# Hybrid decoder layer on one core: both halves of four convolution tiles on one weight, the triangular inverse over fewer elements, compressed probabilities two heads at a time, the second norm's sums taken from PSUM

## The chip, the cores and the metric

The kernel runs on one core of a Trainium2 chip. The metric is the device time of one execution in microseconds (us). The engines are named as the profile names them: PE is TensorE's matmul queue and PEld its weight loads, DVE is VectorE, ACT is ScalarE, POOL is GpSimd, SP is SyncE, whose queue (SPq) issues nearly all DMA transfers. Each engine runs its instructions in order.

## The reference, cut to what matters

One layer over 1024 tokens of width 1024, in float32:

```python
h = rmsnorm(x, norm_mix)
q, kv, gate, qkv_gdn, z, b, a = split(h @ w_in)
o_nsa = rmsnorm(nsa_mixer(q, kv, gate, ...), nsa_norm)   # 8 heads, 2 key/value heads, width 64
o_gdn = gdn_mixer(qkv_gdn, z, b, a, ...)                 # 4 heads, width 128, chunks of 64
x = x + concat([o_nsa, o_gdn]) @ w_out
u = causal_dwconv(rmsnorm(x, norm_ffn) @ ffn_up, ffn_conv)     # width 2 x 2816
x = x + (silu(u_gate) * u_up) @ ffn_down
return rmsnorm(x, norm_final)

# in nsa_mixer, for each query and head: compressed, selected and window attention
o = gate_c * (p_cmp @ vc) + gate_s * (p_sel @ v_sel) + gate_w * (p_win @ v_win)
# in gdn_mixer: q, k, v = split(silu(causal_dwconv(qkv, conv_w))); for each chunk of 64 tokens
a_mat = tril(kb @ k.T * decay, -1)
sol = triangular_solve(a_mat + eye, [vb, kb * exp(g)])   # then a recurrence from chunk to chunk
```

`vc` and the compressed keys have 63 rows (blocks of 32 tokens at a stride of 16), so a compressed probability row has 64 columns here.

## The kernel before, in words

Matrix products keep float32 accuracy by splitting each operand into a high part (ScalarE, a cast) and a low part (the rest, GpSimd or VectorE), and by three products high x high, high x low, low x high (`mm3`, L126 to L128; `mm_more`, L1116). `split_weight` loads 128 x 1024 weights as w_raw and makes w_h on ScalarE (L116) and w_l on GpSimd (L118).

The order on each engine is that of the program text, except that blocks of the program marked with a high priority are moved ahead by the scheduler. The stages, in us of the profiled span:

- to 110: first norm, values and gates, first convolution blocks.
- 110 to 440: `conv_block` (one for each of 12 tiles of 128 channels and each half of 512 tokens, L463 to L469: matmuls into proj_ps, ScalarE copies, three taps and a gate on VectorE) beside gated DeltaNet. DeltaNet goes by pairs of token tiles (4 pairs): `gdn_blocks` (L339 to L355) inverts the 32 x 32 triangular blocks of a pair (2 tiles, 4 blocks, 4 heads) on VectorE. It loads the blocks as bb through DRAM (d_blk), starts from zinit and does 31 passes, each a multiplication into ztmp (L348) and an addition into zb (L350). The 128 partitions are 32 blocks times 4, and each holds 8 of the 32 rows of its inverse; `na` of them take part in pass j. zb goes to DRAM (d_z) and from there to Zx (`gdn_solve`), with which TensorE goes on to the recurrence (L408 to L419).
- 440 to 775: attention in 16 units (8 token tiles, 2 key/value heads). Scores (s_ps, L809, L811), softmax, transposes of the probabilities (pt, L877), copies of these (pT, L880, L882), and products with the values into one tile po of PSUM (L890), which has one buffer and is copied to oT by ScalarE (L893). A unit's compressed probabilities pc are the first of its jobs.
- 775 to 800: output projection and residual (`phase_out`).
- 800 to 870: second norm for the second half of the tokens (`norm_second`). The up projection takes a 2 x 2 block form with seven products in place of eight: its right operands are D (four parts of the normed activations) and T (sums and differences of those). For the first two of 22 tile pairs the plain form runs (`plain`), on D and T3 alone, which covers the making of T0 to T2 (`late`, with `add`, L1075 and L1076, and `split`, L1070 and L1071). Weight sums ss are made on VectorE (L1153), op_h and op_l of them by `split` (L1140, L1142), and the weights themselves are loaded as w_raw (L1134) into memory that the scratch of `norm_second` holds until it is closed.
- 870 to 1254: up projection, convolutions, gate; the result goes to DRAM (d_a).
- 1254 to 1469: down projection (`phase_down`), by pairs of rows js: a_raw (L1301) loaded and split into d_op, w_down quarters b and the residual x1 (xr) loaded two entries of `queue` behind each a_raw (`fetch`, L1294), and matmuls into dn_ps (L1314). Each pair needs 24 matmuls: two rows, four token tiles, three products.

## Time and profile before

| | |
|---|---|
| median of 3 runs | 1486.92 us (1484.90 to 1490.70) |
| profiled execution | 1485.12 us, its span 1483.3 us |
| mean granted TensorE clock | 0.98 |
| PE busy | 1423.7 us, 96% |
| DVE busy | 1090.7 us, 74% |
| ACT busy | 688.1 us, 46% |
| POOL busy | 557.5 us, 38% |

The span is the part of an execution between its first and last instruction. Busy time is the time in which an engine has at least one instruction running. Matmuls overlap one another and their ends are modelled, so the time of one is longer than the step from one to the next.

### The profile page before, as it was taken

The page shows a single profiled execution, that of the slowest core. Times are in us where ns is not written, and L with a number is a line of the kernel's source. Part 1 is how long each engine was busy: PE and PEld are TensorE (multiplying, and loading weights), DVE is VectorE, ACT ScalarE, POOL GpSimd, SP SyncE. Part 2 cuts the span into 40 slices and gives each one's busy share as a digit, 9 for nine tenths or more (in the row PEclk, how much of TensorE's full clock was granted, in tenths as well). Part 3 has the DMA queues.
Part 4 walks back from the last instruction along what each step waited for, and adds up shares of the span by engine and source line. Part 5 has one row for each costly group of instructions (what it writes and reads, how often), then busy time and mean ns, then how long its engine had stood idle before and what let it go on. Part 6 is the DMA issues. An engine that isn't in the chain of part 4 may idle for free.

```text
span 1483.3 us, 21381 instructions
## 1 busy us (share of the span) xinstructions
PE 1423.7 (96%) x7572; PEld 1144.8 (77%) x7572; DVE 1090.7 (74%) x2098; ACT 688.1 (46%) x1347; POOL 557.5 (38%) x547
## 2 busy tenths in 40 slices
...
GB/s 236 87 154 183 110 163 76 116 116 151 77 240 202 169 132 120 104 52 36 65 93 199 1 113 100 107 100 98 88 106 107 107 79 236 265 243 89 96 107 149
DMA packets 105627, 188.06 MB, mean 127 GB/s; under 512 B 17168, under 2 KB 52016, under 8 KB 105392
## 3 DMA queue, kind: packets, MB, share of 16 engines
...
q8 instruction: 60, 0.98, 0.3%
q14 instruction: 47, 0.39, 0.1%
HBM read 135.00 MB, written 51.66 MB: 126 GB/s over the span
## 4 chain that ended last, share of the span: by engine, by line
PE 67%; DVE 16%; DMA 6%; issue 4%; ACT 4%; POOL 2%; SPq 0%; DVEq 0%; ACTq 0%; POOLq 0%
PE up_ps L1116 27%; PE dn_ps L1314 10%; PE po L890 4%; PE pt L877 4%; DVE cv_acc L465 3%; PE proj_ps L128 2%; PE proj_ps L126 2%; PE proj_ps L127 2%; PE s_ps L809 2%; PE s_ps L811 2%; DVE zb L350 1%; DVE ztmp L348 1%; PE og_ps L126 1%; PE og_ps L127 1%; PE og_ps L128 1%
## 5 line engine op out<-in xcount | busy, mean ns | idle before, releaser
L1314 PE MATMUL dn_ps<-d_op 128*128 128x512 f32 x924 | 213.9, 393 | 4.5 <-ACT d_op L1305 1.9
L1314 PEld LDWEIGHTS dn_ps<-d_op 128*128 128x128 f32 x924 | 174.8, 190 | 43.1 <-DVE d_op L1308 2.6
L128 PE MATMUL proj_ps<-hH,w_l 128*128 128x512 f32 x384 | 157.2, 409 | 6.9 <-POOL w_l L118 6.9
L126 PE MATMUL proj_ps<-hH,w_h 128*128 128x512 f32 x384 | 155.5, 407 | 3.6 <-ACT cv_acc L463 3.3
L127 PE MATMUL proj_ps<-hL,w_h 128*128 128x512 f32 x384 | 154.9, 403 | 0.0
L1306 POOL TENSOR_TENSOR d_op<-a_raw,d_op 128x1024 fp32r<-128x1024 f32 (+1 forms) x42 | 105.1, 2504 | 124.0 <-ACT d_op L1305 104.8
L1116 PE MATMUL up_ps<-th,op_h 128*128 128x512 f32 x336 | 133.3, 398 | 11.8 <-ACT op_h L1140 11.8
L1116 PE MATMUL up_ps<-tl,op_h 128*128 128x512 f32 x336 | 133.3, 397 | 0.0
L1116 PE MATMUL up_ps<-th,op_l 128*128 128x512 f32 x336 | 132.7, 396 | 0.0
L118 POOL TENSOR_TENSOR w_l<-w_raw,w_h 128x1024 fp32r<-128x1024 f32 (+2 forms) x46 | 109.5, 2386 | 53.5 <-ACT w_h L116 51.9
L1308 DVE TENSOR_TENSOR d_op<-b,d_op 128x1024 fp32r<-128x1024 f32 (+1 forms) x42 | 81.9, 1954 | 49.2 <-ACT d_op L1307 43.3
L1116 PE MATMUL up_ps<-dh,op_h 128*128 128x512 f32 x288 | 113.0, 398 | 1.4 <-ACT op_h L1140 1.4
L1116 PE MATMUL up_ps<-dl,op_h 128*128 128x512 f32 x288 | 113.7, 396 | 0.0
L1116 PE MATMUL up_ps<-dh,op_l 128*128 128x512 f32 x288 | 110.4, 395 | 0.0
L1228 DVE SCALAR_TENSOR_TENSOR ga<-f_g,vec,ga 128x1024 f32<-128x1024 f32 x44 | 91.0, 2068 | 11.1 <-ACT ga L1226 10.4
L1161 POOL MEMSET f_u<- 128x2 f32 x22 | 2.2, 100 | 253.0 <-DVE acc L1228 160.3
L128 PEld LDWEIGHTS proj_ps<-hH,w_l 128*128 128x128 f32 x384 | 74.1, 193 | 27.0 <-POOL w_l L118 10.9
L1140 ACT ACTIVATE op_h<-w_raw 128x1024 fp32r<-128x1024 f32 (+1 forms) x64 | 58.8, 923 | 71.8 <-PE up_ps L1116 69.9
L465 DVE SCALAR_TENSOR_TENSOR cv_acc<-cv_raw,vec,cv_acc 128x512 f32<-128x512 f32 x72 | 76.6, 1063 | 18.4 <-ACT cv_acc L463 17.6
L126 PEld LDWEIGHTS proj_ps<-hH,w_h 128*128 128x128 f32 x384 | 74.0, 193 | 19.4 <-ACT cv_acc L463 4.7
L1305 ACT ACTIVATE d_op<-a_raw 128x1024 fp32r<-128x1024 f32 (+1 forms) x42 | 41.3, 985 | 101.7 <-PE dn_ps L1314 47.8
L127 PEld LDWEIGHTS proj_ps<-hL,w_h 128*128 128x128 f32 x384 | 74.2, 193 | 15.6 <-DVE hL L188 0.4
...
## 6 DMA issues: line engine op xcount, KB each, us to landing
w_raw<-in_w_up_dram SPq DMA_DIRECT2D x44, 512.0 KB, 3.3
a_raw<-d_a SPq DMA_DIRECT2D x35, 512.0 KB, 3.6
w_raw<-in_w_gdn_dram SPq DMA_DIRECT2D x24, 512.0 KB, 3.7
...
b<-in_w_down_dram SPq DMA_DIRECT2D x20, 512.0 KB, 6.6
...
mg<-d_mix SPq DMA_DIRECT2D x16, 512.0 KB, 3.9
```

Source lines behind the costliest of these rows:

```text
L118: (low or nc.gpsimd).tensor_tensor(out=wl, in0=raw, in1=wh.bitcast(F32), op=ALU.subtract)
L126: nc.tensor.matmul(out, ah, bh, start=(i == 0), stop=False)
L127: nc.tensor.matmul(out, ah, bl, start=False, stop=False)
L128: nc.tensor.matmul(out, al, bh, start=False, stop=(i == n - 1))
L465: nc.vector.scalar_tensor_tensor(out=acc, in0=raw[:, j:j + 512], scalar=tap(j), in1=acc, op0=ALU.mult, op1=ALU.add)
L877: nc.tensor.transpose(pt[0:kk, h, :], src[h], K.ident)
L890: last = nc.tensor.matmul(po[64 * par:64 * par + 64], v, pT[:, par::2], start=(last is None or first), stop=(left == 0))
L1116: mm = lambda a, b, start, stop: nc.tensor.matmul(out, a, b, start=start, stop=stop, skip_group_check=not first)
L1228: nc.vector.scalar_tensor_tensor(out=a, in0=raw[:, j:j + SEQ], scalar=tap(j), in1=a, op0=ALU.mult, op1=ALU.add)
L1306: nc.gpsimd.tensor_tensor(out=al, in0=raw, in1=ah.bitcast(F32), op=ALU.subtract)
L1308: nc.vector.tensor_tensor(out=bl, in0=b[js.start], in1=bh.bitcast(F32), op=ALU.subtract)
L1314: one = lambda a, b, start, stop: nc.tensor.matmul(ps, a, b, start=start, stop=stop, skip_group_check=not first)
```

## The change

It combines edits in several stages.

- `proj_block`: the products with w_h come first, those with w_l last.
- The convolution blocks: tiles 0 to 7 for the first half, then tiles 8 to 11 for both halves with one split weight, then tiles 0 to 7 for the second half.
- `gdn_blocks`: row 4a + r of an inverse stands in partition group r as its a-th row (before: row 8r + a, with the four r of a block in neighbouring partitions), so that pass j needs j // 4 + 1 of the 8 rows in every partition. d_z has another layout, of which a partition's rows are written as eight runs of 32 floats (before: one run of 256); bb is loaded by four transfers.
- `compress` and `values`: vc becomes a block diagonal, two copies of the 64 x 64 values in a 128 x 128 tile for each key/value head; two heads' compressed probabilities are transposed at once, copied by VectorE as pcT and multiplied in one product ahead of the other jobs.
- `phase_out`: its high and low parts stand in a buffer of the attention's pool, two PSUM pools wait by tile, and four copies b11 are added on ScalarE.
- `norm_second`: the differences come from PSUM by scalar_tensor_tensor; the sixteen additions are gone. The splits are T1 on VectorE, then T0 and T2 on GpSimd.
- `phase_down`: the residual is loaded in pieces of two token tiles by 512 columns, two early and six at the end of the queue.

```diff
-    rho = i % 4
+    rho = i // 32
     for a in range(8):
-        c[i, C_ZI + a * 32 + 8 * rho + a] = 1.0
+        c[i, C_ZI + a * 32 + 4 * a + rho] = 1.0
...
-    mm3(K.nc, ps, [(wh[:, k * P:(k + 1) * P], wl[:, k * P:(k + 1) * P], K.hH[:, k, d], K.hL[:, k, d])
-                   for k in range(NK)])
+    jobs = [(wh, h, k) for k in range(NK) for h in (K.hH, K.hL)] + [(wl, K.hH, k) for k in range(NK)]
+    for n, (w, h, k) in enumerate(jobs):
+        K.nc.tensor.matmul(ps, w[:, k * P:(k + 1) * P], h[:, k, d], start=(n == 0), stop=(n == len(jobs) - 1))
...
-    nc.sync.dma_start(bb, bc(db.rearrange("t b h j i -> (t b h) j i"), 1, 4))
+    for r in range(4):
+        nc.sync.dma_start(bb[32 * r:32 * r + 32], db.rearrange("t b h j i -> (t b h) j i"))
     z = K.gt.tile([P, 8, 32], F32, name="zb", tag="zb")
     nc.vector.tensor_copy(z, K.zinit)
     for j in range(31):
-        na, n = min(8, j + 1), 31 - j
+        na, n = j // 4 + 1, 31 - j
...
-    nc.sync.dma_start(dz.rearrange("t b h (r a) i -> (t b h r) (a i)", a=8), z.rearrange("p a i -> p (a i)"))
+    nc.sync.dma_start(dz.rearrange("(a r) t b h i -> (r t b h) a i", r=4), z)
...
-        for ct in range(12):
-            conv_block(K, ct, 0)
-        for ct in range(12):
-            conv_block(K, ct, 1)
+        for cts, bs in ((range(8), (0,)), (range(8, 12), (0, 1)), (range(8), (1,))):
+            for ct in cts:
+                w = split_weight(K, A["w_gdn"][ct], low=None)
+                for b in bs:
+                    conv_block(K, ct, b, w)
...
-            nc.scalar.activation(K.vc[:, h], vp, AF.Copy, scale=0.5)
+            for d in (slice(0, 64), slice(64, 128)):
+                nc.scalar.activation(K.vc[d, h, d], vp, AF.Copy, scale=0.5)
...
-    jobs = [([pc[:, h, :] for h in range(4)], K.vc[:, g, :], 64)]
+    pt = K.p_t.tile([P, 2, P], F32, name="pt", tag="pt")
+    for j in range(2):
+        nc.tensor.transpose(pt[:, j], pc[:, 2 * j:2 * j + 2, :].rearrange("p h n -> p (h n)"), K.ident)
+    pT = K.apl.tile([P, 2, P], F32, name="pcT", tag="pcT", bufs=1)
+    nc.vector.tensor_copy(pT, pt)
+    last = nc.tensor.matmul(po, K.vc[:, g], pT, start=True, stop=False)
+    yield
+    jobs = []
...
-                mh = xp.tile([P, 4, P], F32R, name="mh", tag="mh")
-                ml = xp.tile([P, 4, P], F32R, name="ml", tag="ml")
+                mg = K.og.tile([P, 4, 2 * P], F32R, name="mg", tag="mg", bufs=2)
+                mh, ml = mg[:, :, 0:P], mg[:, :, P:2 * P]
...
+                def put(k, ps):
+                    g = K.vec[:, V_NFFN + k:V_NFFN + k + 1]
+                    put_parts(K, *K.D[k // 4][k % 4], ps, g)
+                    if k < 4:
+                        nc.scalar.activation(K.b11[k], ps, AF.Copy, scale=g)
...
-    def add(out, x, j, k, op0, op1):
-        nc.vector.tensor_tensor(out=out, in0=x, in1=K.D[j][k][0].bitcast(F32), op=op0)
-        nc.vector.tensor_tensor(out=out, in0=out, in1=K.D[j][k][1].bitcast(F32), op=op1)
     def put(k, ps):
         g = K.vec[:, V_NFFN + k:V_NFFN + k + 1]
+        diff = lambda out, x: nc.vector.scalar_tensor_tensor(out=out, in0=ps, scalar=g, in1=x, op0=ALU.mult, op1=ALU.subtract)
         if k < 4:
             put_parts(K, *K.T[3][k], ps, g)
             b12[k] = scr("b12", 4)
             nc.scalar.activation(b12[k], ps, AF.Copy, scale=g)
+            diff(t0[k], K.b11[k])
             return
         k -= 4
         put_parts(K, *K.D[2][k], ps, g)
-        s2 = s1[k] = scr("s1", 4)
-        nc.vector.scalar_tensor_tensor(out=s2, in0=ps, scalar=g, in1=b12[k], op0=ALU.mult, op1=ALU.subtract)
+        s1[k] = scr("s1", 4)
+        diff(s1[k], b12[k])
+        diff(b12[k], t0[k])
...
     def late():
-        for k in range(4):
-            split(2, k, s1[k])
-            add(b12[k], b12[k], 0, k, ALU.subtract, ALU.subtract)
-            split(0, k, b12[k])
-            add(s1[k], s1[k], 0, k, ALU.add, ALU.add)
-            split(1, k, s1[k])
+        for j, src in ((1, b12), (0, t0), (2, s1)):
+            K.T[j] = parts(j)
+            for k in range(4):
+                split(j, k, src[k])
...
-    queue = [(t[js.start], src) for t, js, src in b[0] + b[1]] + [(xr[:, i], K.d_x1[i]) for i in range(NT)]
+    res = lambda r, c: [(xr[:, i:i + 2, 512 * c:512 * c + 512],
+                         K.d_x1[i:i + 2, :, 512 * c:512 * c + 512].rearrange("i p c -> p i c"))
+                        for i in (4 * r, 4 * r + 2)]
+    queue = [(t[js.start], src) for t, js, src in b[0] + b[1]]
+    queue[6:6] = res(0, 0)
     queue += [(t[js.start], src) for p in zip(b[2], b[3]) for t, js, src in p]
+    queue += res(1, 0) + res(1, 1) + res(0, 1)
...
-    K.vc = cp.tile([64, 2, 64], F32, name="vc")
+    K.vc = cp.tile([P, 2, P], F32, name="vc")
+    nc.gpsimd.memset(K.vc, 0.0)
...
-    K.d_z = [dp.tile([2, 4, 4, 32, 32], F32, name=f"d_z{i}") for i in range(2)]
+    K.d_z = [dp.tile([32, 2, 4, 4, 32], F32, name=f"d_z{i}") for i in range(2)]
...
+        K.h3 = {1: mk("h31")}
+        K.b11 = [sum_tile(K, 1, k, "l", F32) for k in range(4)]
```

VectorE in the second norm, before: the end of the part that reads the norm's transposes nt_ps, then the additions. b12 and s1 are the scratch tiles, dh and dl the parts of D.

```order
L1075 TENSOR_TENSOR b12_8835<-b12_8835,dh00_8454 128x512
L188 SCALAR_TENSOR_TENSOR dl23_8477<-nt_ps_8876,vec_68,dh23_8476 128x512
L1088 SCALAR_TENSOR_TENSOR s1_8883<-nt_ps_8876,vec_68,b12_8847 128x512
L1075 TENSOR_TENSOR b12_8839<-b12_8839,dh01_8456 128x512
L1075 TENSOR_TENSOR s1_8856<-s1_8856,dh00_8454 128x512
L1075 TENSOR_TENSOR b12_8843<-b12_8843,dh02_8458 128x512
L1076 TENSOR_TENSOR b12_8835<-b12_8835,dl00_8455 128x512
L1075 TENSOR_TENSOR s1_8865<-s1_8865,dh01_8456 128x512
L1075 TENSOR_TENSOR b12_8847<-b12_8847,dh03_8460 128x512
L1075 TENSOR_TENSOR s1_8874<-s1_8874,dh02_8458 128x512
L1076 TENSOR_TENSOR b12_8839<-b12_8839,dl01_8457 128x512
L1076 TENSOR_TENSOR s1_8856<-s1_8856,dl00_8455 128x512
```

The same place after the change (th20 to th23 hold b12 less b11 until they are split):

```order
L1096 SCALAR_TENSOR_TENSOR b12_8762<-nt_ps_8780,vec_68,th20_8691 128x512
L188 SCALAR_TENSOR_TENSOR dl23_8419<-nt_ps_8810,vec_68,dh23_8418 128x512
L1096 SCALAR_TENSOR_TENSOR s1_8817<-nt_ps_8810,vec_68,b12_8777 128x512
L1096 SCALAR_TENSOR_TENSOR b12_8767<-nt_ps_8790,vec_68,th21_8692 128x512
L1096 SCALAR_TENSOR_TENSOR b12_8772<-nt_ps_8800,vec_68,th22_8693 128x512
L1092 TENSOR_TENSOR tl10_8941<-b12_8762,th10_8940 128x512
L1096 SCALAR_TENSOR_TENSOR b12_8777<-nt_ps_8810,vec_68,th23_8694 128x512
L1092 TENSOR_TENSOR tl11_8943<-b12_8767,th11_8942 128x512
L1092 TENSOR_TENSOR tl12_8945<-b12_8772,th12_8944 128x512
L1092 TENSOR_TENSOR tl13_8947<-b12_8777,th13_8946 128x512
L1122 TENSOR_TENSOR ga_9071<-dh10_8404,th10_8940 128x512
L1122 TENSOR_TENSOR ga_9077<-dh11_8406,th11_8942 128x512
```

The additions L1075 and L1076, twelve of which follow the rows shown, are gone; the splits of T1 (tl10 to tl13) come directly behind the reads of PSUM.

SP's queue at the start of the down projection, before: d_a is the gated activation, x1 the residual, b2 and b3 quarters of w_down.

```order
L1301 DMA a_raw_12296<-d_a1_94 128x1024
L1244 DMA d_a6_99<-so4_12016 128x512
L1294 DMA x1_12050<-d_x1_92 128x1024 x6
L1301 DMA a_raw_12329<-d_a1_94 128x1024
L1294 DMA x1_12050<-d_x1_92 128x1024 x2
L1301 DMA a_raw_12362<-d_a1_94 128x1024
L1294 DMA b2_0_12072<-in_w_down_dram 128x2x512
L1294 DMA b3_0_12084<-in_w_down_dram 128x2x512
L1301 DMA a_raw_12395<-d_a1_94 128x1024
L1294 DMA b2_2_12076<-in_w_down_dram 128x2x512
L1294 DMA b3_2_12085<-in_w_down_dram 128x2x512
```

And after:

```order
L1316 DMA b2_2_12019<-in_w_down_dram 128x2x512
L1261 DMA d_a6_100<-so4_11959 128x512
L1316 DMA x1_11993<-d_x1_93 128x2x512 x2
L1323 DMA a_raw_12272<-d_a1_95 128x1024
L1316 DMA b2_4_12020<-in_w_down_dram 128x2x512
L1316 DMA b3_0_12027<-in_w_down_dram 128x2x512
L1316 DMA b3_2_12028<-in_w_down_dram 128x2x512
L1316 DMA b3_4_12029<-in_w_down_dram 128x2x512
L1323 DMA a_raw_12305<-d_a1_95 128x1024
L1316 DMA b2_6_12021<-in_w_down_dram 128x2x512
L1316 DMA b3_6_12030<-in_w_down_dram 128x2x512
L1323 DMA a_raw_12338<-d_a1_95 128x1024
```

Before, eight rows of the residual are issued in two bursts between three loads of a_raw; after, two pieces stand there, and behind the next a_raw four pieces of w_down follow each other.

TensorE near the end of attention, before, the end of one unit (po_8214):

```order
L877 MATMUL pt_8303<-ident_70,p_sel_8127 128x128 x4
L904 MATMUL nrm_ps_8260<-ones_83,sq_8222 128x1
L877 MATMUL pt_8327<-ident_70,pc_8045 64x128 x4
L809 MATMUL s_ps_8287<-kst01_4406,qT_7750 128x128
L811 MATMUL s_ps_8287<-kst01_4406,qT_7750 128x128
L809 MATMUL s_ps_8292<-kst01_4406,qT_7750 128x128
L811 MATMUL s_ps_8292<-kst01_4406,qT_7750 128x128
L890 MATMUL po_8214<-pT_8308,vst_4409 64x256 x2
L890 MATMUL po_8214<-pT_8258,vst_4409 64x256 x2
L890 MATMUL po_8214<-pT_8220,vc_82 64x256 x2
L877 MATMUL pt_8334<-ident_70,p_win_8203 128x128
```

And after, the end of one unit (po_8043) and the beginning of the next (po_8163):

```order
L904 MATMUL po_8043<-pT_8070,vst_4400 64x256 x2
L891 MATMUL pt_8251<-ident_70,p_sel_8078 128x128 x4
L873 MATMUL pt_8273<-ident_70,pc_7999 128x128 x2
L891 MATMUL pt_8279<-ident_70,p_win_8152 128x128 x4
L876 MATMUL po_8163<-pcT_8167,vc_82 128x256
L904 MATMUL po_8163<-pT_8256,vst_4400 64x256 x2
L904 MATMUL po_8163<-pT_8206,vst_4400 64x256 x2
```

The compressed probabilities take two transposes instead of four, and their product opens po instead of closing it; in this place two groups of transposes of probabilities, ten in all, lie between the last product of one po and the first of the next.

## Rows read from the trace of the kernel before

**Rows 1.** The table of stretches: a stretch of the span in us, then for each engine its busy time in it and (x) its instructions, the mean granted TensorE clock, the DMA engines' busy share, GB/s.
```profile
110.00:235.00 125.00, 112.71 (x576) 86.33 (x577) 116.55 (x280) 47.60 (x100) 54.15 (x44) 0.95 0.46 145
235.00:350.00 115.00, 112.73 (x785) 93.62 (x783) 90.04 (x267) 37.23 (x113) 44.01 (x43) 1.00 0.41 120
350.00:440.00 90.00, 84.38 (x518) 70.33 (x517) 36.37 (x67) 28.08 (x77) 38.17 (x36) 0.94 0.47 148
...
490.00:775.00 285.00, 279.70 (x1937) 212.88 (x1936) 190.49 (x707) 184.56 (x501) 143.28 (x208) 0.99 0.32 93
775.00:800.00 25.00, 24.73 (x126) 20.78 (x125) 13.29 (x24) 11.13 (x19) 10.00 (x15) 1.00 0.62 221
...
853.00:870.00 17.00, 3.83 (x11) 2.28 (x10) 17.00 (x18) 8.57 (x12) 9.79 (x8) 0.66 0.25 93
870.00:1254.00 384.00, 384.00 (x1643) 308.93 (x1642) 323.00 (x333) 176.77 (x216) 64.16 (x59) 1.00 0.31 109
1254.00:1330.00 76.00, 71.49 (x301) 57.41 (x299) 57.29 (x34) 28.86 (x31) 33.87 (x13) 0.96 0.76 273
```

**Rows 2.** What TensorE waited for, over the whole span: waiting instruction <- what ended the wait, us in total, times, longest.
```profile
PE up_ps L1116 <- ACT op_h L1140: 13.2, 2, 11.8
PE proj_ps L128 <- POOL w_l L118: 6.9, 9, 2.0
```

**Rows 3.** VectorE's groups of instructions in 110 to 235: line, operation, tile, shapes, count | busy us, mean ns | idle just before them and what ended it.
```profile
L465 DVE SCALAR_TENSOR_TENSOR cv_acc<-cv_raw,vec,cv_acc 128x512 f32<-128x512 f32 x45 | 46.5, 1034 | 4.9 <-ACT cv_acc L463 4.6
L348 DVE TENSOR_TENSOR ztmp<-zb,bb 128x112 f32<-128x112 f32 (+29 forms) x62 | 26.7, 430 | 1.0
L350 DVE TENSOR_TENSOR zb<-zb,ztmp 128x112 f32<-128x112 f32 (+29 forms) x62 | 22.2, 359 | 1.1
```

**Rows 4.** GpSimd's largest group in 110 to 235, same columns.
```profile
L118 POOL TENSOR_TENSOR w_l<-w_raw,w_h 128x1024 fp32r<-128x1024 f32 x15 | 37.0, 2466 | 17.3 <-ACT w_h L116 17.3
```

**Rows 5.** Two shapes of the inverse's multiplication, over the whole span, same columns with shapes kept apart.
```profile
L348 DVE TENSOR_TENSOR ztmp<-zb,bb 128x192 f32<-128x192 f32 x4 | 1.4, 355 | 0.0
...
L348 DVE TENSOR_TENSOR ztmp<-zb,bb 128x8 f32<-128x8 f32 x4 | 0.7, 171 | 0.1
```

**Rows 6.** DMA issues of the whole span by tile: queue, operation, count, KB each, median us from issue to landing.
```profile
a_raw<-d_a SPq DMA_DIRECT2D x35, 512.0 KB, 3.6
...
kq<-d_kqv SPq DMA_DIRECT2D x8, 512.0 KB, 5.1
...
d_blk<-B SPq DMA_DIRECT2D x32, 16.0 KB, 1.5
d_z<-zb SPq DMA_DIRECT2D x4, 128.0 KB, 3.4
```

**Rows 7.** What VectorE waited for, over the whole span, columns as in rows 2.
```profile
DVE zb L344 <- DMA d_z<-zb: 3.1, 1, 3.1
```

**Rows 8.** TensorE's instructions in order of time, near the end of attention: start us, us until the modelled end of the last one, line, operation, tile, tile sizes, shapes, count.
```profile
758.80 0.60 PE L877 MATMUL pt<-ident,pc 128*64 128x128 f32 x4
...
770.84 0.82 PE L890 MATMUL po<-pT,vst 128*64 128x256 f32 x6
771.59 0.65 PE L890 MATMUL po<-pT,vc 64*64 64x256 f32 x4
772.17 0.51 PE L127 MATMUL og_ps<-w_l,mg 128*128 128x512 f32 x1
```

**Rows 9.** ScalarE's instructions in order of time, same columns, with the idle time before and what ended it in brackets.
```profile
772.28 0.39 ACT L893 ACTIVATE oT<-po 128x256 f32<-128x256 f32 x1 [6.21 <-PE po L890]
```

**Rows 10.** VectorE's groups in 800 to 853, columns as in rows 3.
```profile
L188 DVE SCALAR_TENSOR_TENSOR dl<-nt_ps,vec,dh 128x512 fp32r<-128x512 f32 x8 | 5.7, 744 | 6.0 <-ACT dh L187 6.0
L1075 DVE TENSOR_TENSOR s<-s,dh 128x512 f32<-128x512 f32 x4 | 4.9, 1232 | 0.0
L1076 DVE TENSOR_TENSOR b<-b,dl 128x512 f32<-128x512 f32 x4 | 4.9, 1229 | 0.0
L1075 DVE TENSOR_TENSOR b<-b,dh 128x512 f32<-128x512 f32 x4 | 4.7, 1166 | 0.0
...
L1076 DVE TENSOR_TENSOR s<-s,dl 128x512 f32<-128x512 f32 x4 | 3.7, 954 | 0.0
...
L1088 DVE SCALAR_TENSOR_TENSOR s<-nt_ps,vec,b 128x512 f32<-128x512 f32 x4 | 3.0, 739 | 0.0
```

**Rows 11.** What the queue of DMA issues waited for in 790 to 880, columns as in rows 2.
```profile
SPq L1134 <- DVE tl L1071: 40.1, 1, 40.1
```

**Rows 12.** The chain of work that ended last, 800 to 880: start us, us, engine, tile, line.
```profile
823.72 0.66 DVE s L1088
...
856.22 1.58 DVE ss L1153
...
864.78 2.00 ACT op_h L1140 x2
```

**Rows 13.** GpSimd's instructions in order of time, second norm.
```profile
840.71 3.22 POOL L1071 TENSOR_TENSOR tl<-b,th 128x512 fp32r<-128x512 f32 x2 [1.99 <-ACT th L1070]
```

**Rows 14.** The queue of DMA issues in order of time, start of the down projection.
```profile
1279.46 3.14 SPq L1294 DMA_DIRECT2D x<-d_x  x6
```

**Rows 15.** The chain of work that ended last, 1270 to 1340.
```profile
1286.24 11.05 DMA a_raw<-d_a
```

**Rows 16.** One stretch at the start of the down projection, columns as in rows 1.
```profile
1280.00:1320.00 40.00, 36.27 (x146) 28.64 (x146) 27.58 (x17) 13.31 (x14) 17.84 (x7) 0.91 0.95 353
```

56 lines of the change are left out of this document (28 added, 28 removed).

## The prediction

> **What bounds the kernel now.** I read the table of stretches first [rows 1], then TensorE's waits [rows 2], then in each stretch where TensorE loses time the rows of the engine that it waits for. TensorE is busy nearly everywhere, so the table is read for what it does not do: idle time is stretch less busy, and a granted clock under 1.00 says that part of the busy time ran slower than it could. In 870 to 1254 it is busy 384.00 of 384.00 us at clock 1.00: nothing off TensorE's path can pay there. Time is lost in four places:
> - 110 to 235 (convolutions and the first two pairs of DeltaNet tiles): 125 - 112.71 = 12.3 us idle, and 0.05 x 112.71 = 5.6 us by the clock, 17.9 in all. VectorE has 116.55 of 125 and sets the pace; TensorE also waits for GpSimd's w_l, 6.9 us in nine waits over the whole span.
> - 235 to 440: 2.3 + 5.6 us idle.
> - 853 to 870: 13.2 us idle of 17, clock 0.66. TensorE's largest wait is in it, 13.2 us for op_h, 11.8 of them at once.
> - 1254 to 1330: 4.5 us idle and 0.04 x 71.49 = 2.9 by the clock, 7.4. At clock 1.00 and without idling it would be over that much sooner.
>
> In 490 to 775 (attention) it is busy 279.70 of 285: what is won there must be TensorE work taken away.
>
> **The change, part by part.**
>
> *Projections and convolutions.* Within a block the eight products with w_l now come last, so GpSimd's split may land 16 matmuls later; a matmul of 512 columns takes 384.00 / 1643 = 0.234 us [rows 1], so that is 3.7 us of slack, against a split of 2.47 us [rows 4] and a mean wait of 0.8 [rows 2]. I take these waits as gone. Channel tiles 8 to 11 are split once for both halves, so 24 splits become 20. The inverse does 1560 elements per partition and pass where it did 3156 (the sum over j of na times n). From the rows by form, 8 elements take 171 ns and 192 take 355: 1.0 ns an element [rows 5]. So 1596 x 1.0 ns x 2 operations = 3.2 us less per pair, 6.4 for the two pairs in 110 to 235.
>
> What is a split less worth to VectorE? Its rows in this stretch are stretched [rows 3]: cv_acc takes 1034 ns where a scalar_tensor_tensor of the same 512 elements takes 739 elsewhere [rows 10], 0.295 x 45 = 13.3 us. Undisturbed, ztmp and zb would take 62 x 2 x 0.163 + 2 x 2 x 3156 x 1.0 ns = 32.8 us; they take 26.7 + 22.2 = 48.9, so 16.1 more. That is 29.4 us over GpSimd's 54.15 busy ones [rows 1], 0.54 per us, so 1.3 per split and 5.4 for four. VectorE is relieved of 6.4 + 5.4 = 11.8 us where it sets the pace. I take 10 of TensorE's 17.9 here, since both engines also wait on other things.
>
> Pairs 2 and 3 save the same 6.4 us of VectorE, but it has 90.04 of 115 and 36.37 of 90 busy there, so only what stands on the chain between tiles counts: 3 of the 7.9 idle. Against it: d_z is written in pieces of 128 bytes instead of 1 KB. The write of 128 KB takes 3.4 us now; below it stand 16 KB, which already go in 128-byte pieces, with 1.5 (d_blk), above it 512 KB with 5.1 (kq) [rows 6]. I take 5, that is 1.6 more for each pair; zb has waited for it once, 3.1 us [rows 7], and VectorE has other work then. **Sum of this part: 13, from 5 to 18.**
>
> The Trainium skill, "DMA: Bandwidth & Descriptors", section Specifications, says that transfers under 512 bytes go below line rate because the engine reads, modifies and writes. By it the new write would be the costly one, which is the second rival below; no row here has 128 KB in such pieces.
>
> *Attention.* For each of 16 units two transposes of 128 x 128 replace four of 128 x 64. Four of those take 0.60 us, of which a matmul's modelled end is 0.28, so (0.60 - 0.28) / 3 = 0.11 each [rows 8]: 0.22 saved. The product with vc now is one over the whole array. Before, its four instructions of 64 x 64 tiles ran from 771.59 to the next start at 772.17: 0.58 us. Six instructions of 256 columns before them ran from 770.84 to 771.59, 0.125 each; two such passes are 0.25, so 0.33 saved. 16 x (0.22 + 0.33) = 8.8. At worst the new product costs what the old did (0.58), and 16 x 0.22 = 3.5 is left, less small waits. I take 8, from 2 to 10. VectorE's extra copies stay under 190.49 of 285 busy.
>
> The Trainium skill, "TensorEngine Tiling (Array Packing)", section Overview, speaks against this edit: a product that contracts over 64 or fewer underuses the array, and 64 x 64 tiles run up to twice as fast. By it the old form would have been the cheap one, and the edit would be worth the transposes alone, 3.5. The row disagrees: four tile products took 0.58 us, 0.145 each, no less than passes over 128 rows.
>
> *Output projection.* I cost it at nothing: TensorE is busy 24.73 of 25 us in 775 to 800, and the four new copies go to ScalarE, 11.13 of 25 busy there. Uncovered they would cost some 0.6 us each, an estimate from the 0.39 us of a copy half as wide [rows 9].
>
> *Second norm.* Sixteen additions leave VectorE: 4.9 + 4.9 + 4.7 + 3.7 = 18.2 us [rows 10]. Eight scalar_tensor_tensor join, four of them before the D2 tiles arrive, where VectorE idles 6.0 us before dl, and four after, 4 x 0.74 = 3.0. VectorE comes 15.2 us earlier to the sums of weights, ss, that op_h is made from. op_h starts at 864.78 and ends about 865.8, which ends TensorE's 11.8 us wait, so TensorE stopped at 854.0 [rows 2, 12]. 864.8 - 15.2 + 1.0 = 850.6: before TensorE runs dry. What is late next? The weights themselves: their load waited 40.1 us for the scratch that VectorE's last tl freed [rows 11]; now it waits for GpSimd's last split of T2. Eight splits of 1.61 us, at worst all queued when the last s1 is done at 824.4, end at 837.3, and 512 KB land 3.6 later (a_raw's median), 840.9 [rows 6, 12, 13]. VectorE reaches ss at 856.2 - 15.2 = 841.0. It fits, with three us to spare at TensorE. So the 13.2 us go, and about one more that the clock of 0.66 cost: **14, from 10 to 15.**
>
> *Down projection.* Eight residual rows of 512 KB are issued in two bursts between three a_raw loads; the one behind them took 11.05 us to land, where its median is 3.6 [rows 6, 14, 15]. 4.2 MB at the 353 GB/s of that stretch are 11.9 us [rows 16]. Afterwards only two pieces, 3.0 us, stand there, and the other six come last. But the quarters of w_down move up: four of 512 KB now stand between two a_raw loads, 2.1 MB or 5.9 us, while TensorE needs 24 x 0.234 = 5.6 us for one pair. **5 of the 7.4, from 1 to 7.**
>
> The sum: 13 + 8 + 14 + 5 = 40. The profiled execution took 1485.12 us, so 1445; it was 1.8 below the median of the runs, 1486.92, so **1447** against that.
>
> **The rivals.**
> - *The relief of VectorE is not what holds TensorE in 110 to 235.* For it: 5.6 us of that loss is clock, and VectorE also idles there (8.5 us), mostly behind ScalarE. Against it: no engine is fuller. Only 3 of the 13 come: 1457.
> - *d_z in small pieces becomes the wait.* If the pieces go at the rate of d_blk's, 128 KB take 8 x 1.5 = 12 us, 8.6 more per pair. In pairs 0 and 1 VectorE has convolutions to do meanwhile; pairs 2 and 3 would show it, 17 us: 1464. Against it: d_z's 128 KB, eight times d_blk's 16 KB, take 3.4 us now, little over twice as long, so the time does not go by the bytes. The rule of the Trainium skill ("DMA: Bandwidth & Descriptors", Specifications) would have it go this way.
> - *The stall at 853 only moves.* If TensorE waits for the weights' load or op_l instead, 4 of the 14 come: 1457. It needs the load 13 us later than my worst case.
> - *More is freed.* With all 17.9 us in 110 to 235 and 7 in 235 to 440, 12 more than in my sum: 1435.
> - *Slower.* The new product opens po early, while po has one buffer: on TensorE, in order, po<-pcT stands before the transposes and scores of its own unit, and waits until ScalarE has copied the unit before to oT. That copy takes 0.39 us and ScalarE was waiting for po when it came [rows 9], so a wait forms only where less TensorE work than that lies between; in the shortest place ten transposes do, 1.1 us. If ScalarE's queue held it up, sixteen waits would have to average 2.5 us to eat the 40; from there the kernel is slower, at 3.5 us by 16: 1503. ScalarE is busy 184.56 of 285 us, which speaks against it.
>
> **How the numbers follow.** Forecast (1440 to 1453) 0.60; more freed 0.12; relief not on the path 0.13; small pieces 0.06; stall moves 0.05; po waits 0.04. The range leaves out the po waits and the ends of the outer cases: 1432 to 1464. Half a per cent, 7.4 us, is about what a measurement can tell from no change. Faster by more: 0.93. Within: 0.04 (two bad cases together, or po waits near 2.5 us). Slower: 0.03.
>
> **What would show it.** Right: in 110 to 235 no waits for w_l, mean cv_acc still near 1 us, ztmp and zb together some 6 us less for a pair of pairs; no wait for op_h over 2 us and the up products continuous from 800; pt<-pc 32 times, po<-pcT a quarter us a unit; a_raw near 1285 landing in about 6 us. Wrong: a wait of TensorE for oT at po<-pcT, of VectorE for Zx or d_z over 3 us in each pair, or of ss for its load.

## The result and the profile after

The changed kernel takes 1465.28 us, median of four runs (1463.46 to 1466.99), against 1487.72 (1484.90 to 1490.70) for the kernel before, measured again beside it: a ratio of 0.9849, 95% interval 0.9825 to 0.9872. It is faster by 22 us. The forecast was 40 us and a range that ended at 1464: the direction was right, the size was not. The profiled execution took 1466.07 us with a span of 1463.8.

The table of stretches of the changed kernel answers to [rows 1] (same columns: stretch, its length, busy time and instructions of PE, PEld, DVE, ACT, POOL, granted clock, DMA share, GB/s; the stretches are shifted so that they hold the same work):

```profile
108.00:226.00 118.00, 105.91 (x573) 82.94 (x571) 105.08 (x269) 45.72 (x97) 47.28 (x41) 0.99 0.44 135
226.00:340.00 114.00, 111.43 (x775) 92.52 (x774) 83.82 (x274) 35.01 (x109) 42.73 (x42) 1.00 0.39 113
340.00:428.00 88.00, 86.21 (x547) 72.30 (x547) 37.91 (x67) 29.08 (x80) 38.53 (x33) 0.98 0.52 161
478.00:763.00 285.00, 273.28 (x1868) 214.79 (x1868) 197.22 (x729) 180.68 (x491) 143.93 (x208) 0.99 0.33 97
763.00:788.00 25.00, 25.00 (x125) 20.61 (x122) 12.34 (x23) 11.71 (x21) 7.38 (x13) 1.00 0.51 182
840.00:862.00 22.00, 18.03 (x61) 12.81 (x60) 22.00 (x20) 9.58 (x13) 10.04 (x9) 0.84 0.20 65
862.00:1235.00 373.00, 373.00 (x1600) 300.18 (x1600) 310.83 (x324) 172.77 (x210) 60.10 (x56) 1.00 0.31 109
1235.00:1311.00 76.00, 71.38 (x304) 58.20 (x303) 61.40 (x39) 28.11 (x31) 33.36 (x13) 0.96 0.78 276
```

Two stretches still lose TensorE what the forecast had taken back: attention has 285 - 273.28 = 11.7 us idle where [rows 1] had 285 - 279.70 = 5.3, and the start of the down projection still has 4.6 idle. What TensorE waited for over the whole span (as [rows 2]) says on whom:

```profile
PE pt L891 <- DVE og L950: 7.5, 5, 2.9
PE dn_ps L1336 <- DVE d_op L1330: 4.5, 1, 4.5
PE s_ps L815 <- DVE nmax L829: 3.7, 4, 2.2
PE up_ps L1133 <- ACT op_h L1157: 2.2, 1, 2.2
```

The 11.8 us wait for op_h and all waits for w_l are gone. In their place stand a wait of the probabilities' transposes (pt) for a sum og on VectorE, which was 1.3 us before, and one of the down projection for d_op.

To see where the time came from, I cut both spans at TensorE's marks: last start of a projection matmul (proj_ps), first of the output projection (out_ps), first of the up projection (up_ps), first and last of the down projection (dn_ps). All are starts in the view by tile; what follows the last dn_ps is the same 9.4 us in both. Microseconds of TensorE's program by stage, with the term of the forecast:

| stage | before | after | difference | forecast |
|---|---|---|---|---|
| to the last projection | 467.2 | 455.8 | -11.4 | -13 |
| attention, to the first out_ps | 306.6 | 307.7 | +1.1 | -8 |
| output projection, to the first up_ps | 26.3 | 25.5 | -0.8 | 0 |
| second norm, up projection, to the first dn_ps | 450.5 | 443.1 | -7.4 | -14 |
| down projection, to the last dn_ps | 223.3 | 222.3 | -1.0 | -5 |

Each column is one profile. Among the changed kernel and the runs below that share a stage with it, the same program took 451.6 to 460.3 to the last projection, 306.8 to 307.7 in attention, 440.7 to 443.3 in the second norm and up projection, and 221.3 to 223.9 in the down projection. So the first row is good to some 4 us and the others to one or two, and the mark between the first two rows is not sharp (e1 shows it below).

### The profile page after: what moved, and what is told of

Read it like the earlier page. It is cut to its first block, busy times and chain, and to the rows that moved or that the text cites. A ratio compares the mean times of both kernels' runs of the same rounds, so it can differ in the third digit from the quotient of the medians.

```text
span 1463.8 us, 21239 instructions
## 1 busy us (share of the span) xinstructions
PE 1411.0 (96%) x7508; PEld 1143.5 (78%) x7508; DVE 1069.3 (73%) x2100; ACT 683.3 (47%) x1339; POOL 547.1 (37%) x544
## 4 chain that ended last, share of the span: by engine, by line
PE 75%; DVE 14%; issue 4%; DMA 3%; POOL 2%; ACT 2%; SPq 0%; DVEq 0%; ACTq 0%; POOLq 0%
PE up_ps L1133 27%; PE proj_ps L199 12%; PE dn_ps L1336 11%; PE po L904 3%; PE pt L891 3%; DVE cv_acc L468 2%; PE s_ps L815 2%; PE s_ps L817 2%; PE s_ps L418 1%; PE m_ps L411 1%; PE og_ps L126 1%; PE og_ps L127 1%; PE og_ps L128 1%; DVE zb L353 1%; DVE ztmp L351 1%
## 5 line engine op out<-in xcount | busy, mean ns | idle before, releaser
L118 POOL TENSOR_TENSOR w_l<-w_raw,w_h 128x1024 fp32r<-128x1024 f32 (+2 forms) x42 | 100.0, 2386 | 43.4 <-ACT w_h L116 29.1
L199 PE MATMUL proj_ps<-hH,w_l 128*128 128x512 f32 x384 | 101.6, 398 | 0.0
L1245 DVE SCALAR_TENSOR_TENSOR ga<-f_g,vec,ga 128x1024 f32<-128x1024 f32 x44 | 89.6, 2036 | 12.2 <-ACT ga L1243 11.5
L199 PEld LDWEIGHTS proj_ps<-hH,w_l 128*128 128x128 f32 x384 | 70.6, 188 | 14.6 <-issue 0.8
L468 DVE SCALAR_TENSOR_TENSOR cv_acc<-cv_raw,vec,cv_acc 128x512 f32<-128x512 f32 x72 | 68.2, 947 | 11.8 <-ACT cv_acc L466 10.8
```

The source lines that it names most:

```text
L118: (low or nc.gpsimd).tensor_tensor(out=wl, in0=raw, in1=wh.bitcast(F32), op=ALU.subtract)
L199: K.nc.tensor.matmul(ps, w[:, k * P:(k + 1) * P], h[:, k, d], start=(n == 0), stop=(n == len(jobs) - 1))
L468: nc.vector.scalar_tensor_tensor(out=acc, in0=raw[:, j:j + 512], scalar=tap(j), in1=acc, op0=ALU.mult, op1=ALU.add)
L1245: nc.vector.scalar_tensor_tensor(out=a, in0=raw[:, j:j + SEQ], scalar=tap(j), in1=a, op0=ALU.mult, op1=ALU.add)
```

## Experiments

My theory after the result: each of the three terms that fell well short (attention, second norm, down) met a wait just behind the one removed. Rivals: the parts take time from each other, so that each alone would give its term; or the terms were simply sized too large. The first runs put one part of the change alone into the kernel before; the next take one suspected wait out of the changed kernel. Ratios are to the kernel before on the same chip, with 95% intervals; stage times are from each run's profile, cut as above.

### The parts alone

**e1_front**: projections, convolution order and inverse.

```diff
+    jobs = [(wh, h, k) for k in range(NK) for h in (K.hH, K.hL)] + [(wl, K.hH, k) for k in range(NK)]
+        for cts, bs in ((range(8), (0,)), (range(8, 12), (0, 1)), (range(8), (1,))):
+        na, n = j // 4 + 1, 31 - j
```

> The kernel before with the projection order, the convolution order and the inverse of the change alone. In the changed kernel the last projection matmul comes 11.4 us earlier than before. If these edits earn that by themselves and nothing behind them gives it back, the time is 10 to 13 us shorter (ratio 0.991 to 0.993). If attention, which follows, waits for something that does not come earlier with it, only 5 to 9 us are left.

Measured: 1476.43 against 1485.60, 0.9938 (0.9916 to 0.9960). 9.2 us, less than the 13 forecast: the second case above. In its profile the last projection comes at 452.6, 14.6 us earlier than before, but attention, whose code is unchanged, then takes 311.4, 4.8 more. From 452.6 to 490 TensorE idles 4.9 us at a mean granted clock of 0.91, waiting for nmax (2.5 us) and for a load (mg, 2.1). Part of what the first row gains is given back in the second.

**e2_values**: vc as a block diagonal, compressed probabilities two heads at a time.

```diff
+    nc.vector.tensor_copy(pT, pt)
+    last = nc.tensor.matmul(po, K.vc[:, g], pT, start=True, stop=False)
```

> The kernel before with the block diagonal of vc and the two transposes alone. The prediction's theory, attention is paced by TensorE: 8 us shorter (6 to 9). The rival, VectorE's selection chain and the og sums in its order pace the units, and TensorE reaches the next PSUM buffer earlier only to wait there: 3 us shorter at most, and TensorE's waits for og grow from 1.3 us to 5 or more.

Measured: 1488.45 against 1485.60, 1.0015 (0.9999 to 1.0032); attention 307.4, and TensorE's waits for og grow from 1.3 to 5.3 us, as the rival had it. Worth nothing alone, so no other part took its gain away.

**e3_norm**: the second norm's sums from PSUM, b11 and the order of the splits.

```diff
+            diff(t0[k], K.b11[k])
+        diff(b12[k], t0[k])
```

> The kernel before with the second norm's sums from PSUM alone (and the four b11 copies). The prediction's theory: 14 us shorter. The rival, read from the changed kernel: the wait for ss goes but the next op_h on ScalarE stands behind the last parts of T3, and TensorE waits there and runs at the lower clock level after it: 7 us shorter (6 to 9).

Measured: 1478.32 against 1485.60, 0.9940 (0.9920 to 0.9960); first out_ps to first dn_ps 468.3 where it was 476.8, -8.5: the rival's 6 to 9, not 14. The same wait for op_h, 2.2 us, is left.

**e4_down**: the queue of the down projection.

```diff
+    queue[6:6] = res(0, 0)
+    queue += res(1, 0) + res(1, 1) + res(0, 1)
```

> The kernel before with the new queue of the down projection alone. The prediction's theory: 5 us shorter. The rival, read from the changed kernel: quarters of w_down land earlier, VectorE adds four of them before it makes the next d_op, and TensorE waits 4.5 us for that: 0 to 1.5 us shorter.

Measured: 1483.57 against 1485.60, 0.9986 (0.9971 to 1.0001): 2 us, at the edge of what can be told from nothing. Its stage in the profile is no shorter, 223.4 for 223.3.

By their ratios the four give -9.2 + 2.2 - 8.9 - 2.1 = -18.0 us, where the whole gave -22.4. By the four intervals the sum is good to some 5 us, so the two are not told apart; that the parts eat each other's gain is not seen. The terms themselves fell short.

### Attention

Two questions: what TensorE work the block diagonal saves, and why TensorE waits. TensorE, changed kernel, in order of time: start us, us to the modelled end, line, tile, shapes, count:

```profile
488.53 1.11 PE L891 MATMUL pt<-ident,p_win 128*128 128x128 f32 x4 [2.94 <-DVE og L950]
...
547.10 0.60 PE L876 MATMUL po<-pcT,vc 128*128 128x256 f32 x2
547.54 0.71 PE L891 MATMUL pt<-ident,p_win 128*128 128x128 f32 x5
```

The new product is one matmul in the program but a float32 matmul runs as two passes (x2): 547.54 - 547.10 = 0.44 us, 0.22 a pass. I had priced a pass at 0.125, from [rows 8], where six instructions of 256 columns took 0.75 us. Those were products with 64 columns of the array each (128*64), which go in pairs to po's two halves: in the single records of the trace two of them start 0.007 us apart, the next two 0.21 to 0.27 later. A pass over the whole array costs nearly twice as much, 0.22, close to the 0.234 of a split pass of 512 columns, which fits two halves running side by side. Summed over the 16 units from each start to the next, the products with vc went from 9.28 to 7.1 us (a wait of 1.0 us behind the last one left out) and the transposes of pc from 6.57 to 3.5. In five units the next matmul's modelled start lies only 0.03 us behind the second pass, so 7.1 may be up to 1 us too low: 4 to 5 us are saved, not 8.8. The Trainium skill, "TensorEngine Tiling (Array Packing)", section Overview, has small tiles run up to twice as fast, by which the edit would have been worth the transposes alone, 3.5 us. I had rejected it. The trace gives 3.1 us for the transposes, and on the product it does not agree with the page, since the four tile products took 0.58 us where the whole array takes 0.44; but the sum, 4 to 5, is nearer to that 3.5 than to my 8.8.

The rest is the wait. VectorE at the wait of 2.94 us above, and, two units later, VectorE and TensorE at one of 0.95:

```profile
487.79 0.68 DVE L950 TENSOR_TENSOR og<-og_ps,og 128x512 f32<-128x512 f32 x1
488.39 0.41 DVE L875 COPY pcT<-pt 128x256 f32<-128x256 f32 x1
...
540.30 0.42 DVE L875 COPY pcT<-pt 128x256 f32<-128x256 f32 x1
...
545.66 0.93 DVE L777 TENSOR_TENSOR_SCAN cnt<-eq 128x16 f32<-128x16 f32 x1
...
548.45 0.69 DVE L950 TENSOR_TENSOR og<-og_ps,og 128x512 f32<-128x512 f32 x1
549.20 0.55 PE L891 MATMUL pt<-ident,p_win 128*128 128x128 f32 x3 [0.95 <-DVE og L950]
```

pt and og_ps share the three buffers of one PSUM pool, so a transpose cannot begin until VectorE has read an older og_ps; and on VectorE, in order, that read stands behind the selection's chain of small instructions (L760 to L782). In four of the five waits for og a copy pcT also stands ahead of the read, 8 to 9 us earlier with VectorE hardly idle between; at the longest, 2.94 us, it stands behind. The chain itself is stretched: cnt takes 0.93 us here, while GpSimd multiplies p_sel, and 0.18 at 574.34. How much of the waits that makes, no run tells apart.

The change does not simply add 16 copies to VectorE. Before, it copied 44 tiles pT, 16 of them the transposes of pc (64 rows). After, it copies 16 pcT, and since the count n that deals out the copies starts one job later, 38 other pT instead of 28: 26.1 + 6.7 = 32.8 us for 30.0. 7.5 - 1.3 = 6.2 us more waiting for og eats the 4 to 5 saved; the difference has the sign of the table's +1.1, though other waits changed too (nmax from 2.1 to 3.7).

**e5_no_values**: the changed kernel with the old values and transposes.

```diff
-    last = nc.tensor.matmul(po, K.vc[:, g], pT, start=True, stop=False)
+    jobs = [([pc[:, h, :] for h in range(4)], K.vc[:, g, :], 64)]
```

> The changed kernel with the old form of the compressed values (64 x 64 tiles, four transposes, their product last) put back, all else as changed. If that edit is worth what it was worth by itself (2 us lost), the time is 1 to 3 us below the changed kernel's 1465 us: 1462 to 1464. If it is worth something once the stages ahead are faster, the time is above: 1467 to 1472.

Measured: 1462.75 against 1487.29, 0.9843 (0.9820 to 0.9866); attention 306.4. Not told apart from the changed kernel: this edit is worth nothing here either. TensorE's waits for og are 3.0 us.

**e6_act_copy**: the changed kernel, pcT copied by ScalarE.

```diff
-    nc.vector.tensor_copy(pT, pt)
+    nc.scalar.activation(pT, pt, AF.Copy)
```

> The changed kernel, but pcT is copied by ScalarE instead of VectorE. If VectorE's added copies (16 of 0.41 us) are what makes og and the units late, TensorE's waits for og fall from 7.5 us to under 4 and the time is 3 to 6 us below 1465. If the whole-array product is the cost (0.47 us a unit instead of 0.25), the time stays within 2 us of 1465 and po<-pcT still takes 0.21 us or more a pass.

Measured: 1458.24 against 1487.29, 0.9809 (0.9784 to 0.9833); attention 299.3 where the changed kernel has 307.7. TensorE's wait, and the copy in its new place:

```profile
PE pt L891 <- DVE og L950: 4.5, 5, 1.4
541.00 0.37 ACT L875 ACTIVATE pcT<-pt 128x256 f32<-128x256 f32 x1
```

So pcT's place on VectorE, not the product, kept the gain: the product still takes 0.22 us a pass. Waits fell by 3.0 for og and 1.3 for nmax, together 4.3 of the 8.4 us of the stage. The last projection comes 4.5 us later in this profile (460.3); to the first out_ps the gain is 763.5 - 759.6 = 3.9 us, near those waits. By the ratios it is some 6 us. The stage itself repeats: 299.3, 301.0 (e11) and 300.4 (e15) with pcT on ScalarE.

**e14_before_act**: the kernel before, its copy of the compressed probabilities moved to ScalarE. Is e6's gain the move alone?

```diff
-            if n % 4 in (0,):
+            if n % 4 in (0,) and n:
```

> The kernel before, with the copy of each unit's transposed compressed probabilities on ScalarE instead of VectorE, and nothing else. If VectorE's copies alone are what the attention waits for, this gives the 7 us that the same move gave in the changed kernel: 1478 to 1481. If the move is worth that only where TensorE has less to do (two transposes and a cheaper product), it gives 0 to 3 us: 1483 to 1486.

Measured: 1483.68 against 1486.31, 0.9986 (0.9968 to 1.0004); attention 302.9, -3.7. In time it is 2.6 us, within the 0 to 3 of the second case, and not told apart from nothing. By the stage times, one profile each, the edit alone gives +0.8 (e2), the move alone -3.7, both -7.3 (e6). So far as these tell, the block diagonal pays only once VectorE is out of its way.

### Second norm and up projection

First stall: op_h, which TensorE waited for 11.8 us [rows 2], is now in time. ScalarE, changed kernel, in order of time (start, us, line, tile, shapes; idle before and what ended it in brackets):

```profile
837.70 1.07 ACT L1157 ACTIVATE op_h<-ss 128x1024 fp32r<-128x1024 f32 x1 [0.74 <-DVE ss L1170]
...
847.80 0.64 ACT L1091 ACTIVATE th<-ga 128x512 fp32r<-128x512 f32 x1 [2.74 <-DVE ga L1124]
850.51 0.63 ACT L1091 ACTIVATE th<-ga 128x512 fp32r<-128x512 f32 x1 [2.07 <-DVE ga L1124]
851.05 1.04 ACT L1157 ACTIVATE op_h<-w_raw 128x1024 fp32r<-128x1024 f32 x1
```

op_h<-ss starts at 837.70, 48.7 us after the first up_ps (789.0); before it was 864.78 [rows 12], 64.7 after (800.1). That is 16.0 earlier, where 15.2 was forecast. But before 847.80 and before 850.51 ScalarE idles for ga: this is `late3`, which remakes T3 for the block form (VectorE L1122, GpSimd L1123, VectorE L1124, then th on ScalarE). It stands in ScalarE's order ahead of the next op_h, which starts at 851.05. TensorE, in order of time:

```profile
852.14 0.50 PE L1133 MATMUL up_ps<-dh,op_h 128*128 128x512 f32 x1 [2.16 <-ACT op_h L1157]
...
855.44 0.80 PE L1133 MATMUL up_ps<-dh,op_l 128*128 128x512 f32 x1 [0.39 <-POOL op_l L1159]
```

Its waits there are 2.2, 1.0 and twice 0.4 us, and the mean granted clock is 0.84 in 840 to 862: 4.0 us idle and 0.16 x 18.03 = 2.9 us by the clock.

**e7_no_t3**: the remaking of T3 left out; the products that use it take the old T3.

```diff
-                K.late3(K.last_split)
+                pass
```

> The changed kernel without the remaking of T3 (the products with T3 take the old one, so part of the up projection is left out of what they should hold). If the T3 parts in front of the next op_h on ScalarE are the new wait behind the plain products, TensorE runs through 840 to 862 at clock 1.00, and the time is 6 to 8 us below the changed kernel's 1465: 1457 to 1459. If the weights' loads or op_l are what is late, 1462 to 1466.

Measured: 1455.44 against 1487.29, 0.9789 (0.9766 to 0.9811); first up_ps to first dn_ps 433.5, which is 17.0 less than before. TensorE does not wait at all in 840 to 865:

```profile
840.00:865.00 25.00, 25.00 (x109) 20.29 (x108) 21.12 (x24) 8.46 (x12) 2.60 (x3) 1.00 0.30 110
```

This takes T3's work from VectorE, GpSimd and ScalarE too, none from TensorE. So the 14 of the forecast were there to be had; T3, behind the stall removed, kept 9.6 of the 17. Of these the waits and the clock in 840 to 862 make up 6.9; where the rest lies is open.

**e9_wide**: its scratch in two tiles instead of four, so that it waits less for buffers.

```diff
-            w = row_tile(K, 0)[:, 0:512]
+            if k % 2 == 0:
+                wide = row_tile(K, 0)
+            w = wide[:, 512 * (k % 2):512 * (k % 2) + 512]
```

> The changed kernel, with the four scratch pieces of the new T3 in two tiles instead of four, so that the third piece need not wait for the first tile's low part (VectorE waits 0.98 us there, and T3's high parts come late to ScalarE). If that buffer is what holds the next op_h, 2 to 6 us below 1465. If it is the length of the chain of VectorE, GpSimd and ScalarE itself, within 2 us of 1465.

Measured: 1463.90, 0.9858 (0.9835 to 0.9882); the stage 443.3. No change: buffers were not it.

**e10_t3_later**: with e9's tiles, T3 remade behind the operands of the next tile pair.

The call moves from `plain` to behind `ops = prepare(2)`, and all of `late3`'s operations, not its splits alone, are ordered behind the last split given to it.

```diff
-                K.late3(K.last_split)
...
+            K.late3(K.last_split)
...
+            with tc.issue_after(gps.ins):
+                nc.vector.tensor_tensor(out=w, in0=src[0], in1=src[1], op=ALU.subtract)
```

> The changed kernel, with the new T3 made behind the first seven-product operands (issued after their last low part) instead of ahead of them, its four scratch pieces in two tiles. If the place of T3 in the order of ScalarE and VectorE is the new wait, TensorE runs on from the plain products without a wait for op_h, and 5 to 9 us of the 10 that leaving T3 out gave come: 1456 to 1460. If T3 is then late for its own product, the wait stands some 14 us later and 1462 to 1466 result.

Measured: 1457.88 against 1485.46, 0.9825 (0.9804 to 0.9847); the stage 438.9, 4.2 less than the changed kernel's. TensorE's waits in 800 to 900 go on to the next in line:

```profile
PE up_ps L1136 <- DVE f_u L1173: 2.1, 1, 2.1
PE up_ps L1136 <- POOL op_l L1162: 0.9, 1, 0.9
```

Waits for op_h are gone and the granted clock in 840 to 862 is 1.00, so the place of T3 in the order was part of the cost: the same work, issued later, gives back 4 of the 10 us of the stage (439.0 in e11 and 437.4 in e15 agree). In the whole time that is not told apart from the changed kernel: the intervals, 0.9804 to 0.9847 and 0.9825 to 0.9872, overlap.

### Down projection

The chain of work that ended last, changed kernel (start us, us, engine, tile, line), and VectorE and TensorE there in order of time:

```profile
1262.14 6.71 DMA a_raw<-d_a
...
1276.98 3.42 DVE b L1343 x2
1281.39 4.55 DVE b L1343 x2
1285.95 3.30 DVE d_op L1330
```

```profile
1276.90 9.04 DVE L1343 TENSOR_TENSOR b<-b,b 128x1024 f32<-128x1024 f32 x4
...
1289.29 2.93 PE L1336 MATMUL dn_ps<-d_op 128*128 128x512 f32 x6 [4.48 <-DVE d_op L1330]
```

a_raw lands in 6.7 us where it took 11.05 [rows 15], about the 6 forecast. Behind it VectorE is next: four sums of quarters of w_down (b, L1343) stand in its order ahead of d_op. They take 9.04 us, and singly, beside GpSimd's splits for d_op:

```profile
1276.76 2.49 POOL L1328 TENSOR_TENSOR d_op<-a_raw,d_op 128x1024 fp32r<-128x1024 f32 x1 [4.26 <-ACT d_op L1327]
1276.90 3.43 DVE L1343 TENSOR_TENSOR b<-b,b 128x1024 f32<-128x1024 f32 x1
1280.26 1.21 DVE L1343 TENSOR_TENSOR b<-b,b 128x1024 f32<-128x1024 f32 x1
```

Of the 24 sums of L1343 in the changed kernel, six start while a GpSimd instruction runs, and each of them ends 1.08 us after that instruction (here GpSimd's at 1276.76 + 2.49 = 1279.25, the sum at 1280.33); the others take 1.21 to 1.23, the four narrower ones 0.7. Two of the four in question are such: 3.4 us each, where the other two take 1.21. So half of the 9.04 us goes by beside GpSimd's splits. No run moves those away, so what that would give is not known.

**e8_one_sum**: one of the third product's two sums left out; that product then takes the plain quarter.

```diff
-        comb(b11, b12, b11, ALU.add, js)
```

> The changed kernel with one of the two sums of w_down quarters in the third product of the down projection left out (that product then takes the plain quarter). If VectorE's sums ahead of d_op are TensorE's 4.5 us wait there, the wait falls under 1 us and the time is 4 to 7 us below 1465 (wait and lower clock level). If the landing of a_raw or of the quarters is what is late, within 2 us of 1465.

Measured: 1458.17 against 1485.46, 0.9818 (0.9803 to 0.9833); the stage 215.9, 6.4 less, and no wait of TensorE left in 1220 to 1320. This removes work too, but TensorE's 4.5 us wait went with it, as the first case has it. By the ratios (0.9849 for the changed kernel) it is 4.6 us.

### Front

**e12_proj**: projections and convolution order alone.

```diff
+    jobs = [(wh, h, k) for k in range(NK) for h in (K.hH, K.hL)] + [(wl, K.hH, k) for k in range(NK)]
+        for cts, bs in ((range(8), (0,)), (range(8, 12), (0, 1)), (range(8), (1,))):
```

> The kernel before with the projection order and the convolution order alone, without the smaller inverse. The run with both gave 9.2 us. By the prediction's working, w_l's waits (6.1) and four splits less (5.4 of VectorE) make up more than half: 5 to 8 us. If VectorE's elements in the inverse are what counts, 2 to 4 us.

Measured: 1479.15 against 1485.46, 0.9963 (0.9949 to 0.9977): 5.5 us by the ratio, the first case. Its profile is like e1's: 453.0 to the last projection, then 311.4 of attention.

**e13_inverse**: the smaller inverse alone.

```diff
-        na, n = min(8, j + 1), 31 - j
+        na, n = j // 4 + 1, 31 - j
```

> The kernel before with the smaller inverse alone. The prediction counted 6.4 us of VectorE in 110 to 235 and took most of it as TensorE's. If VectorE's elements set the pace there: 4 to 7 us shorter. If what counts is GpSimd's w_l and the chain of transfers through DRAM (bb, d_z, Zx), which the inverse does not shorten: within 2 us of before, though ztmp and zb together take some 6 us less for two pairs.

Measured: 1491.09 against 1486.31, 1.0038 (1.0015 to 1.0061): slower by 4.8, which neither case had.

TensorE's matmuls of the recurrence (m_ps, one view by tile each for the kernel before, e12, e13 and the changed kernel; behind the durations stand the first and last start):

```profile
L408 PE MATMUL m_ps<-S,wq x128: 270/275/378, 220.7 to 412.6; 128*128 128x128 f32 x128
L410 PE MATMUL m_ps<-S,wq x128: 271/275/377, 216.8 to 401.6; 128*128 128x128 f32 x128
L409 PE MATMUL m_ps<-S,wq x128: 271/275/423, 220.3 to 415.7; 128*128 128x128 f32 x128
L411 PE MATMUL m_ps<-S,wq x128: 270/275/554, 212.7 to 402.7; 128*128 128x128 f32 x128
```

The order alone ends the recurrence at 401.6. The inverse with it starts the recurrence 4.1 us earlier (212.7) and ends it no earlier (402.7; in e1 it runs from 212.7 to 401.4). By itself it starts 0.4 earlier and ends 3.1 later, although its multiplications and additions fell, over all pairs, from 48.3 + 42.5 to 39.6 + 40.1 us. In e13's waits a weights' load is new, and most of w_l's is still there:

```profile
PE proj_ps L128 <- POOL w_l L118: 6.0, 8, 2.0
PE cmp_ps L683 <- DMA w_raw<-in_w_dram: 4.1, 1, 4.1
```

Why that load comes late in e13, and whether it explains the 4.8 us, stays open.

### A version that beats both

**e11_both**: e10 and e6 together.

```diff
-    nc.vector.tensor_copy(pT, pt)
+    nc.scalar.activation(pT, pt, AF.Copy)
...
-                K.late3(K.last_split)
...
+            K.late3(K.last_split)
```

> The kernel of the run with T3 made later, with pcT also copied by ScalarE. The two act in stages that follow each other, so their gains should add: 7 for the copy, 5 to 9 for T3, 1449 to 1453 against 1465. If T3 made later gives nothing: 1458.

Measured: 1456.32 against 1485.46, 0.9808 (0.9789 to 0.9826), the changed kernel 0.9849 (0.9825 to 0.9872). It beats the changed kernel by some 6 us, but the forecast of 1449 to 1453 missed: the gains did not add. By the ratio it is where the copy alone is (e6, 0.9809), although the profile has both stages shorter, attention 301.0 and the up projection 439.0. Together with e6 and e15, from which it is not told apart, it is the fastest that keeps all work.

**e15_all_act**: e11, and VectorE left only one of eight of the copies of transposed probabilities.

```diff
-            if n % 4 in (0,):
+            if n % 8 == 7:
```

> The kernel with T3 made later and pcT copied by ScalarE, and nearly all other copies of transposed probabilities on ScalarE too (VectorE keeps every eighth). If VectorE's order still sets the units' pace, 2 to 5 us below that kernel (ratio 0.978 against 0.981). If ScalarE becomes what is waited for, slower than it by 2 us or more.

Measured: 1456.97 against 1486.31, 0.9799 (0.9767 to 0.9831). Not told apart from e11, and attention takes 300.4 for 301.0: no sign that the rest of the copies matter once pcT is on ScalarE, though four runs leave room for the 2 to 5 us forecast. The slower case did not come.

## Why the prediction was right or wrong

- **Front, 13 forecast, 11.4 came by the table, 9.2 alone (e1).** The size was near, its division was not. The waits for w_l went, as said. VectorE's busy time in the first stretch fell by 116.55 - 105.08 = 11.5 us, where 11.8 was forecast:

```profile
L468 DVE SCALAR_TENSOR_TENSOR cv_acc<-cv_raw,vec,cv_acc 128x512 f32<-128x512 f32 x43 | 37.0, 861 | 0.4
L351 DVE TENSOR_TENSOR ztmp<-zb,bb 128x60 f32<-128x60 f32 (+24 forms) x62 | 24.2, 391 | 4.5 <-DMA bb<-d_blk 3.2
L353 DVE TENSOR_TENSOR zb<-zb,ztmp 128x60 f32<-128x60 f32 (+24 forms) x62 | 19.5, 315 | 1.2
```

  ztmp and zb have 43.7 for 48.9 [rows 3], near the 6 us announced, and cv_acc went from 1034 to 861 ns where I had said it stays near 1 us. But TensorE's idle time there is 118 - 105.91 = 12.1 us, as much as before (12.3); the stretch is 7 us shorter by a clock of 0.99 for 0.95 and less busy time. The step that failed is "I take 10 of TensorE's 17.9 here", VectorE's relief turned into TensorE time: the order alone (e12) ends the recurrence as early as order and inverse together and gives 5.5 of the 9.2 us. The inverse by itself loses 4.8; whether it gives the other 3.7 beside the order is not settled, since the intervals of e12 and e1 touch and both reach the first out_ps at 764. So the rival that VectorE's relief is not what holds TensorE was nearer in its mechanism, but not in its price. The price of a split, 0.54 us of VectorE per us of GpSimd, was no rate either: VectorE loses by single meetings (last section).
- **Small pieces of d_z: the rival did not come.** The write takes 3.9 us for 3.4 [rows 6], less than the 5 taken. The Trainium skill's "DMA: Bandwidth & Descriptors", section Specifications, would have transfers under 512 bytes lose by reading, modifying and writing; these medians lean that way by 0.5 us, but they are of four transfers each, and the runs scatter: the old form took 2.0 in e12, the small pieces 3.2 in e13. The wait of zb for d_z comes twice, 6.5 us in all, on VectorE, not on TensorE.
- **Attention, 8 forecast, none came.** The failing step is "two such passes are 0.25, so 0.33 saved": it is 0.44, so 0.58 - 0.44 = 0.14 is saved by the product, and 4 to 5 us in all. And VectorE's copies, costed at nothing because it had 190.49 of 285 busy, delay a read that frees TensorE's buffer: with pcT on ScalarE the stage is some 7 us shorter (e6, e11, e15). How the read is delayed is in part argued, since at the longest wait no pcT stands ahead of it. A busy share does not price an instruction in an in-order queue. The "Slower" rival, po waiting for oT, never formed.
- **Output projection, 0 forecast, -0.8:** right within what a profile tells.
- **Second norm, 14 forecast, 7.4 came.** Every step up to op_h held, to 0.8 us. "What is late next?" was asked of the weights alone; T3's remaking in ScalarE's order was not looked at. This is the rival "the stall at 853 only moves", with another mechanism than its op_l or load; T3 kept 9.6 us of what was to be had (e7).
- **Down, 5 forecast, 1.0 came.** The load of a_raw shortened as forecast. What failed is the step from the shorter load to the end: VectorE's sums behind it, 9.04 us for four, are late next (e8), half of that while GpSimd splits.

The sum with the measured sizes is -11.4 + 1.1 - 0.8 - 7.4 - 1.0 = -19.5, the difference of the spans, 1483.3 - 1463.8. Of the 20 us missing, attention has 9, the second norm 7 and the down projection 4.
